# A hybrid SSD and attention layer on one core: w_down's operands prepared after the products with w_up in the first half, and that half's second norm as two fused VectorE passes

## The chip, the cores and the metric

The kernel runs on one core of a Trainium2 chip. The metric is the device time of one execution in microseconds (us). The comparison is with the median of three runs of the kernel before.

## The reference

One step of a one-layer encoder is computed for a prompt of 2048 frames and a sample of 64 frames, each frame a row of 1024 numbers, all in float32:

```
mix = token_mixers(x)                      # SSD heads and windowed attention, projections w_in and w_out
h = LN1(alpha * x + mix)
y = LN2(alpha * h + (silu(h @ w_gate) * (h @ w_up)) @ w_down)
LN(r) = (r - mean) * rsqrt(var + eps) * g + b
```

w_gate and w_up are 1024 x 2816, w_down is 2816 x 1024. Besides y, the states of both mixers are returned. The change concerns the second half of the layer alone: the preparation of w_down, and LN2 on the first 1024 frames of the prompt.

## The kernel before

Every float32 operand of a large product is split into two float16 parts, a high and a low one, and a product is three TensorE matmuls (`mm3`, lines 127 to 129: high by high, high by low, low by high) into one PSUM bank. Before the split an operand is scaled by a power of two taken from its largest absolute value.

The feed-forward part runs in two halves of the prompt, `h` = 0 (blocks 0 to 3, 256 frames each, two row tiles of 128 frames per block) and `h` = 1 (blocks 4 to 7, with the sample). In each half a loop goes over `p` = 0 to 10, the pairs of 128 columns of w_gate and w_up, which are also pairs of 128 rows of w_down. One pass of the loop (lines 1362 to 1370) has these steps:

- `gate(p)`: seven products of 4 x 3 matmuls with w_gate's operands (a scheme of the Strassen-Winograd kind), then SiLU on ScalarE (ACT).
- `flush(pend)`: the products with w_down for the pass before, `down_rows`. Each of eight rows of 128 frames and each half of the columns has 6 matmuls into a bank `pds`, and VectorE (DVE) adds the bank to the accumulator `acc` in SBUF (line 1198).
- `get_w(h, p + 1, 0)`: in the first half `prep_w` loads the next pair of w_gate columns (1 MB, line 943) into a tile `raw`, takes its bound, and splits it into eight operands (ACT line 954, DVE line 955) that are also stored to HBM (line 956). The second half loads these again (`load_ws`).
- `get_w(h, p, 2)`: `prep_d` loads w_down's rows of this pass (1 MB, line 990), takes the bound, and splits them into the operands `wd`: four in the first half, eight in the second.
- `up(h, p, groups)`: the seven products with w_up, their product with the gate, its bound, and the split into the operands `act` (lines 1143 and 1144).
- `get_w(h, p + 1, 1)`: the next pair of w_up columns.

A bound is taken thus: ACT sums absolute values into a column (line 935), DVE takes the larger of two columns (`am`, line 936) and casts it (line 80), TensorE spreads it over the partitions with a small matmul into the bank `pmx` (line 81, called the max product below), and DVE reduces the bank (line 82) and makes the scale from it (lines 92 to 95).

The raw tiles of w_gate, w_up and w_down share two buffers (`tag="raw", bufs=2`), so that a load waits until the split of the raw tile two loads earlier is done.

When the last pass of the first half has been multiplied with w_down, `last(rows, False)` (line 1281) normalizes the rows of blocks 0 to 3. DVE takes the mean and variance (lines 1296 and 1297) and the reciprocal root (`rsqrt1`, lines 113 to 123), and forms `nb` = -mean * root (line 1301). Then ACT applies scale and bias to the 128 x 1024 row tile (line 1311), DVE multiplies by g (line 1312), and GpSimd (POOL) adds b (line 1313). SyncE (SP) writes the tile out (line 1315) and the same buffer is loaded again for the second half (line 1190). At the end of the second half the rows go through two fused DVE passes instead (lines 1306 and 1308).

The order of the instructions on each engine is made by a scheduler when the program is built, from the order in which the program issues them, a simulated timeline and `tc.high_priority`. On the chip each engine runs its own list strictly in order.

Of the kernel before, what the change touches and what calls it, by code (L numbers as in the profile page):

```python
# [13 lines left out]
F32 = mybir.dt.float32  # L14
U32 = mybir.dt.uint32
I32 = mybir.dt.int32
AF = mybir.ActivationFunctionType
ALU = mybir.AluOpType
# [4 lines left out]
P = 128  # L23
# [26 lines left out]
def layer_kernel(ctx: ExitStack, tc: tile.TileContext, I, O, consts):  # L50
    nc = tc.nc
    V, S, G, T, Q = nc.vector, nc.scalar, nc.gpsimd, nc.tensor, nc.sync

    cp = ctx.enter_context(tc.tile_pool(name="cp", bufs=1))
    small = ctx.enter_context(tc.tile_pool(name="small", bufs=4))
# [29 lines left out]
    def max3():  # L85
        return psx[0].tile([P, P], F32, tag="max", name="pmx")
# [10 lines left out]
    def absmax(out, in_):  # L97
        ax = {2: AX.X, 3: AX.XY, 4: AX.XYZ}[len(in_.shape)]
        V.tensor_reduce(out=out, in_=in_, op=ALU.max, axis=ax, apply_absolute_value=True)
# [809 lines left out]
    def b_tiles(pool_, h, order):  # L909
        return {i: pool_.tile([P, 4, 2, 4, P], F16, tag="B", bufs=len(order), name=f"B{h}_{i}") for i in order}  # L910
# [107 lines left out]
    def scheme(h, p):  # L1018

        return h == 1 and p < NP_ - 2  # L1020

    def load_ws(p, m, order):
        wts[p, m] = w_tiles(p, m, order)
        for i in order:
            Q.dma_start(out=wts[p, m][i], in_=wsd[p][m][i])

    def get_w(h, p, m):
        if p >= NP_:
            h, p = h + 1, 0
        if h == 2:  # L1030
            return
        if m == 2:
            prep_d(h, p)
        elif h == 0:
            prep_w(p, m)
        else:
            load_ws(p, m, ORD + (0,))
# [3 lines left out]
    gb = {}  # L1041
# [15 lines left out]
    def products_sample(w):  # L1057

        ps = psp.tile([P, 2, DSEQ], F32, tag="p", name="pss")
        for f in range(2):  # L1060
            for kk in range(2):
                a = w[((1, 2), (0, 4))[f][kk]]
                for k in range(4):
                    mm3(ps[:, f], a[:, 0, k], a[:, 1, k], sB[:, kk, 0, k], sB[:, kk, 1, k],
                        start=(kk + k == 0), stop=(kk == 1 and k == 3))
        return ps
# [51 lines left out]
    def up(h, p, groups):  # L1118
        iu = invs[:, p, 1:2]
        for g in groups:  # L1120
            am = small.tile([P, 4], F32, tag="ama", name="ama")
            if g.sub:
                o = g.sg
                V.scalar_tensor_tensor(out=o, in0=products_sample(wts[p, 1]), scalar=iu, in1=o,
                                       op0=ALU.mult, op1=ALU.mult)
                absmax(am[:, 0:1], o)
            else:
                s = products(wts[p, 1], g)
                for j, c in enumerate(CS):
                    o = s["5"] if c == "11" else s[c]  # L1130
                    V.scalar_tensor_tensor(out=o, in0=s[c], scalar=iu, in1=g.sg[c], op0=ALU.mult, op1=ALU.mult)
                    absmax(am[:, j:j + 1], o)
                    s[c] = o
                absmax(am[:, 0:1], am)
            asc = small.tile([P, 1], F32, tag="asc", name="asc")
            ai = small.tile([P, 1], F32, tag="ai", bufs=8, name="ai")
            scale_from(am[:, 0:1], ai, asc, 2.0 ** 11 if scheme(h, p) and not g.sub else 2.0 ** 13,
                       ps=max3())
            act = {}
            g.acts[p] = act, ai  # L1140

            def split(at, x):
                S.activation(at[:, 0], x, AF.Identity, scale=asc)  # L1143
                V.scalar_tensor_tensor(out=at[:, 1], in0=x, scalar=asc, in1=at[:, 0], op0=ALU.mult, op1=ALU.subtract)  # L1144

            def put(i, x):
                if g.nq == 4:
                    act[i] = p3r.tile([P, 2, 4, P], F16, tag="act", bufs=7, name="act")
                else:
                    if i % 2:  # L1150
                        two[0] = p3r.tile([P, 2, 2, 2, P], F16, tag="act", bufs=7, name="act2")
                    act[i] = two[0][:, (i - 1) % 2]
                split(act[i], x)

            two = [None]

            if g.sub:
                at = p3r.tile([P, 2, 2, DSEQ], F16, tag="acts", bufs=2, name="acts")
                split(at, o)
                for f in range(2):  # L1160
                    act[f] = at[:, :, f]
                continue

            a11, a12, a21, a22 = s["11"], s["21"], s["12"], s["22"]
            put(1, a11)
            if not scheme(h, p):
                put(2, a12)
                put(3, a21)
                put(4, a22)
                continue  # L1170
            put(4, a22)
            G.tensor_tensor(out=a22, in0=a21, in1=a22, op=ALU.add)
            G.tensor_tensor(out=a21, in0=a11, in1=a21, op=ALU.subtract)
            G.tensor_tensor(out=a11, in0=a22, in1=a11, op=ALU.subtract)
            put(6, a11)
            put(2, a12)
            put(7, a21)
            put(5, a22)
            G.tensor_tensor(out=a12, in0=a12, in1=a11, op=ALU.subtract)
            put(3, a12)  # L1180
# [100 lines left out]
    def last(rows, end):  # L1281

        b, n = rows[0][0], len(rows)
        L = P if b < NB else DSEQ
        mv = small.tile([P, 2, 2], F32, tag="mv", bufs=6, name="mv")[:L]
        rs = small.tile([P, 2], F32, tag="rs2", bufs=6, name="rs2")[:L, :n]
        nb = small.tile([P, 2], F32, tag="nb", name="nb")[:L, :n]
        with tc.high_priority(offset=PRI):
            for j, row in enumerate(rows):
                r = accs[row][:L]  # L1290
                if end and (b == 6 or j == 0 and b != 7):
                    row_stats(r, L, mv[:, j, 0:1], mv[:, j, 1:2])
                else:
                    bs = small.tile([P, 2, 6], F32, tag="bs", name="bs")
                    for c in range(2):
                        V.bn_stats(out=bs[:L, c], in_=r[:, c * 512:c * 512 + 512])
                    V.bn_aggr(out=mv[:, j], in_=bs[:L])
            for j in range(n):
                rsqrt1(mv[:, j, 1:2], LN_EPS / ALPHA ** 2, rs[:, j:j + 1], L)
                if not end:  # L1300
                    V.scalar_tensor_tensor(out=nb[:, j:j + 1], in0=mv[:, j, 0:1], scalar=-1.0, in1=rs[:, j:j + 1],
                                           op0=ALU.mult, op1=ALU.mult)
        for j, row in enumerate(rows):
            r = accs[row][:L]
            if end:
                V.scalar_tensor_tensor(out=r, in0=r, scalar=mv[:, j, 0:1], in1=gb[2][:L, 0],
                                       op0=ALU.subtract, op1=ALU.mult)
                V.scalar_tensor_tensor(out=r, in0=r, scalar=rs[:, j:j + 1], in1=gb[2][:L, 1],
                                       op0=ALU.mult, op1=ALU.add)
            else:  # L1310
                S.activation(r, r, AF.Identity, scale=rs[:, j:j + 1], bias=nb[:, j:j + 1])
                V.tensor_tensor(out=r, in0=r, in1=gb[2][:L, 0], op=ALU.mult)
                G.tensor_tensor(out=r, in0=r, in1=gb[2][:L, 1], op=ALU.add)
            c0 = b * BLK + j * P
            Q.dma_start(out=(O["y_p"].rearrange("b l d -> (b l) d")[c0:c0 + P] if b < NB else
                             O["y_s"].rearrange("b l d -> (b l) d")), in_=r)
# [36 lines left out]
    for h in range(2):  # L1353
        Bt = {**(b_tiles(p3, h, ORD[:5]) if h else B0), **b_tiles(p3r, h, ORD[5:])}
        for i in ORD:
            for q in range(4):
                if h or (q, i) not in direct:
                    Q.dma_start(out=Bt[i][:, q], in_=hd[4 * h + q][i])
        groups = [Group(Bt, blocks(4 * h, 4 * h + 4))]
        if h == 1:  # L1360
            groups.append(Group(sB, [[(NB, 0)]]))
        for p in range(NP_ - 2 if h else NP_):
            gate(p, groups)
            flush(pend)
            get_w(h, p + 1, 0)
            if p or h:
                get_w(h, p, 2)
            up(h, p, groups)
            get_w(h, p + 1, 1)
            pend = (p, groups)  # L1370


    p, p1 = NP_ - 2, NP_ - 1
# [21 lines left out]
    for g in (gs, ga):  # L1395
        for rows in g.rows:
            last(rows, True)
# [53 lines left out]
```

## Time and profile before

| | |
|---|---|
| median of three runs | 2293.24 us (2290.3 to 2294.82) |
| the profiled execution's own time | 2292.77 us |
| span from its first to its last instruction | 2291.0 us |
| TensorE busy | 2166.3 us, 95% |
| VectorE busy | 1778.9 us, 78% |
| ScalarE busy | 1031.2 us, 45% |
| GpSimd busy | 439.6 us, 19% |
| granted clock of TensorE, mean | 0.983 |

The span is 1.77 us shorter than the time of the execution. PE is TensorE, PEld its weight loads. In the trace a line such as L1198 is a line of the kernel before. After "<-" in brackets stands what ended an idle time.

### The profile page before, as it was taken

The page shows a single profiled execution, that of the slowest core. Times are in us where ns is not written, and L with a number is a line of the kernel's source. Part 1 is how long each engine was busy: PE and PEld are TensorE (multiplying, and loading weights), DVE is VectorE, ACT ScalarE, POOL GpSimd, SP SyncE. Part 2 cuts the span into 40 slices and gives each one's busy share as a digit, 9 for nine tenths or more (in the row PEclk, how much of TensorE's full clock was granted, in tenths as well). Part 3 has the DMA queues.
Part 4 walks back from the last instruction along what each step waited for, and adds up shares of the span by engine and source line. Part 5 has one row for each costly group of instructions (what it writes and reads, how often), then busy time and mean ns, then how long its engine had stood idle before and what let it go on. Part 6 is the DMA issues. An engine that isn't in the chain of part 4 may idle for free.

```text
span 2291.0 us, 38739 instructions
## 1 busy us (share of the span) xinstructions
PE 2166.3 (95%) x14805; PEld 1295.6 (57%) x14805; DVE 1778.9 (78%) x4389; ACT 1031.2 (45%) x2040; POOL 439.6 (19%) x388
## 2 busy tenths in 40 slices
PE   5898999999999999989999999999889999999996
PEld 5787778777875555434444444444344444444674
DVE  7786887797778768477777877776987877777978
ACT  5444544554474657644444444432233333333331
POOL 2111211111112002022222222211322222222400
PEclk9899999999999999999999999999999999999998
DMA  7001000100032557643333333345442222222431
GB/s 225 15 26 32 26 19 34 33 24 25 35 98 96 190 170 275 230 146 131 114 126 124 136 132 129 129 163 209 166 144 91 91 87 81 93 81 84 144 109 74
DMA packets 139774, 248.33 MB, mean 108 GB/s; under 512 B 21184, under 2 KB 54212, under 8 KB 139588
## 3 DMA queue, kind: packets, MB, share of 16 engines
q1 hardware_dynamic: 139588, 245.86, 31.9%
q8 instruction: 116, 1.90, 0.3%
q14 instruction: 70, 0.57, 0.1%
HBM read 161.90 MB, written 83.91 MB: 107 GB/s over the span
## 4 chain that ended last, share of the span: by engine, by line
PE 58%; DVE 21%; issue 8%; DMA 6%; ACT 5%; POOL 2%; SPq 0%; DVEq 0%; ACTq 0%; POOLq 0%
PE ps L129 7%; PE ps L127 7%; PE ps L128 7%; PE mm L127 4%; PE mm L129 4%; PE mm L128 3%; DVE w L955 3%; DMA raw<-in_w_up 2%; PE pd L127 2%; PE pd L129 2%; PE pd L128 2%; PE pso L127 2%; PE pso L128 2%; PE pso L129 2%; DVE cc L449 2%
## 5 line engine op out<-in xcount | busy, mean ns | idle before, releaser
L127 PE MATMUL ps<-B,w 128*128 128x512 f16 (+1 forms) x1344 | 486.0, 363 | 14.4 <-ACT a L1086 8.7
L128 PE MATMUL ps<-B,w 128*128 128x512 f16 (+1 forms) x1344 | 487.7, 363 | 0.0
L129 PE MATMUL ps<-B,w 128*128 128x512 f16 (+1 forms) x1344 | 485.0, 363 | 0.0
L128 PEld LDWEIGHTS <-w 128*128 128x128 f16 x2920 | 284.3, 99 | 170.2 <-issue 27.7
L129 PEld LDWEIGHTS <-w 128*128 128x128 f16 x2920 | 284.9, 99 | 157.3 <-issue 8.3
L127 PEld LDWEIGHTS <-w 128*128 128x128 f16 x2920 | 284.5, 99 | 157.7 <-issue 8.9
L127 PE MATMUL mm<-x,w 128*128 128x256 f16 (+1 forms) x1224 | 315.1, 268 | 6.5 <-ACT w L254 2.2
L129 PE MATMUL mm<-x,w 128*128 128x256 f16 (+1 forms) x1224 | 314.8, 268 | 1.3 <-DVE w L257 1.3
L128 PE MATMUL mm<-x,w 128*128 128x256 f16 (+1 forms) x1224 | 315.3, 268 | 0.0
L1198 DVE SCALAR_TENSOR_TENSOR acc<-pds,ai,acc 128x512 f32<-128x512 f32 x208 | 152.8, 742 | 33.9 <-PE pds L129 33.7
L1198 DVE SCALAR_TENSOR_TENSOR acc<-pd,ai,acc 128x512 f32<-128x512 f32 x216 | 151.0, 739 | 26.9 <-PE pd L129 26.0
L955 DVE SCALAR_TENSOR_TENSOR w<-raw,fsc,w 128x512 f16<-128x512 f32 x176 | 150.6, 895 | 20.9 <-ACT w L954 20.9
L127 PE MATMUL pds<-wd,act 128*128 128x512 f16 x416 | 158.1, 380 | 7.4 <-DVE acc L1198 6.5
L128 PE MATMUL pds<-wd,act 128*128 128x512 f16 x416 | 158.1, 380 | 0.0
L129 PE MATMUL pds<-wd,act 128*128 128x512 f16 x416 | 157.4, 380 | 0.0
L1090 POOL TENSOR_TENSOR a<-a 128x512 f32<-128x512 f32 (+1 forms) x48 | 59.6, 1241 | 460.9 <-ACT a L1089 408.7
L1001 ACT ACTIVATE wd<-rawd,fsc 128x512 f16<-128x512 f32 x124 | 83.5, 715 | 138.0 <-PE pd L129 70.6
L954 ACT ACTIVATE w<-raw,fsc 128x512 f16<-128x512 f32 x176 | 114.1, 710 | 66.4 <-POOL raw L963 30.3
L1143 ACT ACTIVATE act<-a,asc 128x512 f16<-128x512 f32 (+1 forms) x123 | 76.4, 683 | 117.1 <-DVE asc L94 111.5
L128 PEld LDWEIGHTS <-act 128*128 128x128 f16 x668 | 65.5, 98 | 87.2 <-issue 14.9
L127 PEld LDWEIGHTS <-act 128*128 128x128 f16 x668 | 65.5, 98 | 81.6 <-ACT act L1143 5.3
L129 PEld LDWEIGHTS <-act 128*128 128x128 f16 x668 | 65.3, 98 | 80.5 <-DVE act L1144 1.8
(378 smaller groups left out, 4331.0 us busy)
## 6 DMA issues: line engine op xcount, KB each, us to landing
w<-ws SPq DMA_DIRECT2D x204, 256.0 KB, 3.0
ws<-w SPq DMA_DIRECT2D x176, 256.0 KB, 2.1
rawd<-in_w_down SPq DMA_DIRECT2D x22, 1024.0 KB, 5.0
x<-in_x_prompt SPq DMA_DIRECT2D x32, 512.0 KB, 4.2
raw<-in_w_gate SPq DMA_DIRECT2D x11, 1024.0 KB, 5.3
raw<-in_w_up SPq DMA_DIRECT2D x11, 1024.0 KB, 5.5
hd<-ht SPq DMA_DIRECT2D x41, 256.0 KB, 2.1
B<-hd SPq DMA_DIRECT2D x41, 256.0 KB, 5.4
```

The costliest lines, as they stand in the source:

```text
L127: T.matmul(out, lh, rh, start=start, stop=False, **kw)
L128: T.matmul(out, lh, rl, start=False, stop=False, **kw)
L129: T.matmul(out, ll, rh, start=False, stop=stop, **kw)
L449: V.scalar_tensor_tensor(out=cc[:, c], in0=cin[:, c, k:k + n], scalar=CW(k, ch + c), in1=cc[:, c], op0=ALU.mult, op1=ALU.add)
L954: S.activation(w[i][:, 0], x, AF.Identity, scale=sc)
L955: V.scalar_tensor_tensor(out=w[i][:, 1], in0=x, scalar=sc, in1=w[i][:, 0], op0=ALU.mult, op1=ALU.subtract)
L1001: S.activation(w[i][:, 0], x, AF.Identity, scale=sc)
L1090: G.tensor_tensor(out=s["7"], in0=s["7"], in1=s["5"], op=ALU.add)
L1143: S.activation(at[:, 0], x, AF.Identity, scale=asc)
L1198: V.scalar_tensor_tensor(out=acc[:, cs], in0=ps, scalar=ai, in1=acc[:, cs], op0=ALU.mult, op1=ALU.add)
```

## The change

Two edits. In the first half, `get_w(h, p, 2)` is issued after `up` and no longer ahead of it (passes 1 to 10; pass 0 has its w_down from ahead of the loop). And `last` always takes the two fused DVE passes, so that `nb`, the ACT pass and the POOL pass go.

```diff
@@ def last(rows, end):
-        nb = small.tile([P, 2], F32, tag="nb", name="nb")[:L, :n]
...
-                if not end:
-                    V.scalar_tensor_tensor(out=nb[:, j:j + 1], in0=mv[:, j, 0:1], scalar=-1.0, in1=rs[:, j:j + 1],
-                                           op0=ALU.mult, op1=ALU.mult)
         for j, row in enumerate(rows):
             r = accs[row][:L]
-            if end:
-                V.scalar_tensor_tensor(out=r, in0=r, scalar=mv[:, j, 0:1], in1=gb[2][:L, 0],
-                                       op0=ALU.subtract, op1=ALU.mult)
-                V.scalar_tensor_tensor(out=r, in0=r, scalar=rs[:, j:j + 1], in1=gb[2][:L, 1],
-                                       op0=ALU.mult, op1=ALU.add)
-            else:
-                S.activation(r, r, AF.Identity, scale=rs[:, j:j + 1], bias=nb[:, j:j + 1])
-                V.tensor_tensor(out=r, in0=r, in1=gb[2][:L, 0], op=ALU.mult)
-                G.tensor_tensor(out=r, in0=r, in1=gb[2][:L, 1], op=ALU.add)
+            V.scalar_tensor_tensor(out=r, in0=r, scalar=mv[:, j, 0:1], in1=gb[2][:L, 0],
+                                   op0=ALU.subtract, op1=ALU.mult)
+            V.scalar_tensor_tensor(out=r, in0=r, scalar=rs[:, j:j + 1], in1=gb[2][:L, 1],
+                                   op0=ALU.mult, op1=ALU.add)
@@ the loop over p
             get_w(h, p + 1, 0)
-            if p or h:
+            if h:
                 get_w(h, p, 2)
             up(h, p, groups)
+            if p and not h:
+                get_w(h, p, 2)
             get_w(h, p + 1, 1)
```

What the scheduler makes of it is seen in the order of the instructions. The first place is DVE in pass 2 of the first half, where w_down's bound is taken and its operands are split; `am_13766` and `a_13773` are the maxima of w_down of that pass. Before:

```order
L1083 TENSOR_TENSOR a<-ps,a 128x512
L955 SCALAR_TENSOR_TENSOR w_3_3_13715<-raw_3_13706,fsc,w_3_3_13715 128x512
L1198 SCALAR_TENSOR_TENSOR acc_1_13093<-pds,ai,acc_1_13093 128x512 x2
L936 TENSOR_TENSOR am_13766<-am_13766 128x1
L80 CAST a_13773<-am_13766 128x1
L1198 SCALAR_TENSOR_TENSOR acc_0_13127<-pds,ai,acc_0_13127 128x512 x2
L82 TENSOR_REDUCE pm<-pmx 128x1
L92 TENSOR_SCALAR pb<-pm 128x1
L94 TENSOR_SCALAR fsc<-pb 128x1
L95 RECIPROCAL invs<-fsc 128x1
L997 TENSOR_SCALAR invs<-invs 128x1
L936 TENSOR_TENSOR am_13935<-am_13935 128x1
```

With the change (`a_13875` is the maximum of the pass's activations, `a_13908` that of w_down, `a_13942` that of the next w_up):

```order
L80 CAST a_13875<-ama 128x1
L80 CAST a_13908<-am_13901 128x1
L80 CAST a_13942<-am_13935 128x1
L1083 TENSOR_TENSOR a<-ps,a 128x512
L1198 SCALAR_TENSOR_TENSOR acc_1_13165<-pds,ai,acc_1_13165 128x512
L82 TENSOR_REDUCE pm<-pmx 128x1
L92 TENSOR_SCALAR pb<-pm 128x1
L94 TENSOR_SCALAR asc<-pb 128x1
L95 RECIPROCAL ai<-asc 128x1
L1144 SCALAR_TENSOR_TENSOR act<-a,asc,act 128x512 x4
L82 TENSOR_REDUCE pm<-pmx 128x1
L92 TENSOR_SCALAR pb<-pm 128x1
```

The cast of w_down's maximum and its max product stood alone in the middle of the products with w_up, close behind the load. They now stand behind the maximum of the activations, and the split of w_down follows the split of the activations. On TensorE the max product of w_down moves in each of the ten passes from 93 to 195 matmuls ahead of that of the activations to 20 to 29 behind it.

The second place is DVE in the norm of the first half, at the second row tile. Before (`nb` feeds ACT, `gb` holds g and b):

```order
L122 SCALAR_TENSOR_TENSOR rsw_18208<-rs_18187,mv 128x1
L1296 BN_STATS bs<-acc_0_13091 128x6
L123 SCALAR_TENSOR_TENSOR rs_18187<-rsw_18208,rs_18187 128x1
L1297 BN_AGGR mv<-bs 128x2
L1301 SCALAR_TENSOR_TENSOR nb<-mv,rs_18187 128x1
L116 TENSOR_SCALAR mv<-mv 128x1
L117 TENSOR_SCALAR rs_18260<-mv 128x1
L119 TENSOR_SCALAR rs_18260<-rs_18260 128x1
L122 SCALAR_TENSOR_TENSOR rsw_18270<-rs_18260,mv 128x1
L123 SCALAR_TENSOR_TENSOR rs_18260<-rsw_18270,rs_18260 128x1
L122 SCALAR_TENSOR_TENSOR rsw_18270<-rs_18260,mv 128x1
L123 SCALAR_TENSOR_TENSOR rs_18260<-rsw_18270,rs_18260 128x1
```

With the change (L1301 and L1303 are the two fused passes in the new file):

```order
L1198 SCALAR_TENSOR_TENSOR acc_0_13091<-pds,ai,acc_0_13091 128x512
L116 TENSOR_SCALAR mv<-mv 128x1
L1301 SCALAR_TENSOR_TENSOR acc_1_13057<-acc_1_13057,mv,gb 128x1024
L1295 BN_STATS bs<-acc_0_13091 128x6
L117 TENSOR_SCALAR rs_18187<-mv 128x1
L1198 SCALAR_TENSOR_TENSOR acc_0_13091<-pds,ai,acc_0_13091 128x512
L119 TENSOR_SCALAR rs_18187<-rs_18187 128x1
L1295 BN_STATS bs<-acc_0_13091 128x6
L122 SCALAR_TENSOR_TENSOR rsw_18206<-rs_18187,mv 128x1
L1296 BN_AGGR mv<-bs 128x2
L123 SCALAR_TENSOR_TENSOR rs_18187<-rsw_18206,rs_18187 128x1
```

The first fused pass needs the mean alone and runs ahead of the root; the second follows when the root is there. Nothing of this norm stands on ACT's and POOL's lists any more.

## Rows read from the trace of the kernel before

**Rows 1.** The page's part 1: busy time, share and instructions of each engine.

```profile
PE 2166.3 (95%) x14805; PEld 1295.6 (57%) x14805; DVE 1778.9 (78%) x4389; ACT 1031.2 (45%) x2040; POOL 439.6 (19%) x388
```

**Rows 2.** Windows by stage: length, busy PE, PEld, DVE, ACT, POOL, clock, DMA.

```profile
1100.00:1589.00 489.00, 485.25 (x2305) 220.50 (x2304) 366.17 (x687) 221.07 (x368) 109.00 (x77) 1.00 0.41 145
1589.00:1690.00 101.00, 84.79 (x484) 38.95 (x483) 99.31 (x209) 31.78 (x45) 37.70 (x20) 0.93 0.45 154
1690.00:2190.00 500.00, 496.53 (x3608) 262.50 (x3607) 394.72 (x732) 165.71 (x277) 119.94 (x93) 1.00 0.31 98
```

**Rows 3.** Waits of PE, 1000 to 1100 us: us in total, times, longest.

```profile
PE pmx L81 <- DVE a L80: 5.1, 2, 3.4
```

**Rows 4.** Timeline around 1088 us, by engine: start, duration, instruction, idle before it.

```profile
1077.11 0.39 SPq L990 DMA_DIRECT2D rawd<-in_w_down  x1
...
1085.85 1.06 ACT L935 ACTIVATE wd<-rawd 128x1024 f16<-128x1024 f32 x1 [5.28 <-DMA rawd<-in_w_down]
...
1088.21 0.16 DVE L936 TENSOR_TENSOR am<-am 128x1 f32<-128x1 f32 x1 [5.27 <-ACT wd L935]
...
1088.62 0.29 PE L81 MATMUL pmx<-ident,a 128*128 128x128 bf16 x1 [3.39 <-DVE a L80]
```

**Rows 5.** Window 1080 to 1100 us, columns as in rows 2.

```profile
1080.00:1100.00 20.00, 16.61 (x72) 7.08 (x70) 10.37 (x23) 8.47 (x15) 1.51 (x1) 0.91 0.49 164
```

**Rows 6.** Waits of PE, 1100 to 1589 us, all of them.

```profile
PE ps L127 <- ACT a L1089: 1.3, 3, 0.5
PE pds L127 <- DVE acc L1198: 1.2, 4, 0.4
PE ps L127 <- ACT a L1086: 1.0, 1, 1.0
```

**Rows 7.** Timeline of PE, two matmuls of 128x512 that follow each other.

```profile
1590.59 0.38 PE L127 MATMUL ps<-B,w 128*128 128x512 f16 x1
1590.81 0.38 PE L128 MATMUL ps<-B,w 128*128 128x512 f16 x1
```

**Rows 8.** Lines 943 and 990, loads of w_gate and w_up, then w_down.

```profile
DMA to landing us min/median/max: 5.1/5.5/8.3
...
DMA to landing us min/median/max: 4.7/5.0/5.8
```

**Rows 9.** Timeline of DVE, the split of w_down in one pass.

```profile
1095.18 2.74 DVE L1002 SCALAR_TENSOR_TENSOR wd<-rawd,fsc,wd 128x512 f16<-128x512 f32 x4 [0.45 <-ACT wd L1001]
```

**Rows 10.** Lines of DVE, 1589 to 1690 us: count, busy us, mean ns, idle before.

```profile
L1312 DVE TENSOR_TENSOR acc<-acc,gb 128x1024 f32<-128x1024 f32 x8 | 9.7, 1217 | 0.1
...
L1301 DVE SCALAR_TENSOR_TENSOR nb<-mv,rs 128x1 f32<-128x1 f32 x8 | 3.2, 404 | 0.0
```

**Rows 11.** Lines of POOL, 1589 to 1690 us, the addition of b.

```profile
L1313 POOL TENSOR_TENSOR acc<-acc,gb 128x1024 f32<-128x1024 f32 x8 | 19.7, 2468 | 41.1 <-DVE nb L1301 22.1 <-DVE acc L1312 12.0 <-issue 4.1
```

**Rows 12.** Timelines of POOL and DVE beside its passes: second; first, second, eighth.

```profile
1613.12 2.34 POOL L1313 TENSOR_TENSOR acc<-acc,gb 128x1024 f32<-128x1024 f32 x1 [4.92 <-DVE acc L1312]
...
1606.42 1.80 DVE L123 SCALAR_TENSOR_TENSOR rs<-rsw,rs 128x1 f32<-128x1 f32 x1
1613.21 2.27 DVE L123 SCALAR_TENSOR_TENSOR rs<-rsw,rs 128x1 f32<-128x1 f32 x1
1670.26 3.49 DVE L1144 SCALAR_TENSOR_TENSOR act<-a,asc,act 128x512 f16<-128x512 f32 x2
```

**Rows 13.** Lines 123 and 1144 over the whole span: ns min/median/max.

```profile
L123 DVE SCALAR_TENSOR_TENSOR rs<-rsw,rs x51: 99/145/2270, 1594.1 to 2283.5; 128x1 f32<-128x1 f32 x48, 64x1 f32<-64x1 f32 x3
...
L1144 DVE SCALAR_TENSOR_TENSOR act<-a,asc,act x123: 464/746/2845, 994.9 to 2263.1; 128x512 f16<-128x512 f32 x107, 128x256 f16<-128x256 f32 x16
```

**Rows 14.** Line 1306, the fused pass at the end of the second half.

```profile
L1306 DVE SCALAR_TENSOR_TENSOR acc<-acc,mv,gb x8: 1264/1270/1272, 2216.8 to 2278.9; 128x1024 f32<-128x1024 f32 x8
```

**Rows 15.** Waits, 1550 to 1720 us and (PE) 1589 to 1690 us.

```profile
ACT acc L1311 <- DVE nb L1301: 27.4, 7, 6.4
...
PE ps L127 <- ACT a L1086: 3.8, 1, 3.8
```

## The prediction

> **What bounds the kernel now.** The page comes first: TensorE is busy 95% of the span, VectorE 78% [rows 1]. These are averages, so the stages that the change touches are read one by one, with the windows. From 1100 to 1589 us, most of the first half's loop, PE is busy 485.25 of 489 us at full clock: TensorE bounds it, and at most 3.75 us are to be had there [rows 2]. From 1589 to 1690 us, where the first half is normalized and the second begins, it is the other way round: PE is busy 84.79 of 101 us at a mean clock of 0.93, and DVE 99.31 of 101 us. DVE bounds this stretch, and PE waits 16.2 us in it. From 1690 us on PE is full again (496.53 of 500), so that whatever is won or lost earlier is carried to the end undiminished.
>
> Next, the waits of PE, stage by stage. From 1000 to 1100 us there are two that matter, 5.1 us together, of the small matmul that spreads a maximum [rows 3]. The timeline of the longer one shows its cause from the first to the last step: SP issues the load of w_down at 1077.11, ACT has waited 5.28 us when it lands at 1085.85, DVE has waited 5.27 us when it takes the maximum, and PE stands 3.39 us at the max product [rows 4]. PE's list is strictly ordered, so a max product that comes early stops everything behind it. The same 20 us have a mean clock of 0.91 where full is 1.00 (the two levels are 2.4 and 1.2 GHz) [rows 5]. From 1100 to 1589 us PE waits only 3.5 us in all, and for no max product [rows 6].
>
> **Part A: w_down behind the products with w_up.** Each of the ten moved steps issues one load on SP, the bound on ACT and DVE, one max product on PE, four splits on ACT and four on DVE; nothing on POOL in this half. No instruction is added. What changes is the places in the lists.
>
> What goes: both waits of rows 3 belong to w_down's max product, which now stands 20 to 29 matmuls behind that of the activations. The load is long done there. Gain 5.1 us. With the wait goes the fall of the clock behind it: 0.09 of 20 us below full means 3.6 us at half rate, by the two levels, and so 1.8 us of lost work if PE had been at it all the time; part of these 3.6 us it only waited, so I take half, 0.9 us. Together **-6.0 us**.
>
> What is late next: first, the split itself. By the order, w_down's first product follows its max product after 20 to 27 matmuls. Two matmuls stand 0.22 us apart [rows 7], so that is 4.3 to 5.8 us. In that time DVE makes the scale (about 1 us), finishes up to four splits of the activations, and makes the first split of w_down; four splits take 2.74 us and start 0.45 us behind ACT [rows 9]. That is 1 + 2.7 + 1.2 = 4.9 us at the worst: short by 0.6 us or with 0.9 us to spare. Second, the two raw buffers: the next w_gate load now waits for this split. From w_down's max product to w_gate's there are 72 to 77 matmuls, 15.5 to 16.6 us. The chain is the scale 1 us, the splits 3.2 us, the issue 0.4 us, the load, two sums on ACT of some 1.1 us each, and maximum and cast 0.4 us; with the load at its median of 5.5 us [rows 8] that is 12.7 us, and up to a microsecond more if DVE is still at the activations. With the slowest load, 8.3 us, it is 15.5 to 16.5 us and PE would begin to wait. Behind a waiting max product on PE stands all work; behind a late bound on DVE stand the additions that free PSUM banks for PE.
>
> So the new waits are bounded by nothing and by about 1.5 us in each of ten passes, 15 us. The nearest row is the loop as it stands, where loads of the same size run through a chain of the same kind and no max product waits [rows 6]. I stay near the low end, **+2.0 us**.
>
> **Part B: two fused passes.** Eight row tiles. DVE loses eight multiplications, 9.7 us, and eight `nb` of about 0.14 us where nothing is in their way, 1.1 us [rows 10]. It gets sixteen fused passes of 1.27 us, priced by the same pass at the end of the second half [rows 14]: 20.3 us. On paper that is +9.5 us on the engine that bounds.
>
> The trace has another cost of the old way. While POOL adds b, 2.34 us from 1613.12, an operation of DVE on one number per partition takes 2.27 us [rows 12], where the median of its kind is 0.145 us [rows 13]. It begins with POOL's pass and ends with it. Beside each of POOL's eight passes one or more DVE operations are stretched so, of kinds that otherwise take 0.15 to 0.7 us; the first is stretched to 1.80 us, and the last pair, two splits, to 3.49 us where two take some 1.4 [rows 12, 13]. Over what their kinds take elsewhere the eight are 1.6 to 2.2 us too long, 15.5 us in all. POOL's passes are 19.7 us [rows 11], which is the most that they can have cost; below, I allow 0.7 us each, a third of what is seen, if the delay would otherwise come from something else.
>
> The Trainium skill (SBUF — State Buffer, section Who interferes with whom) says that GpSimd shares one pair of SBUF ports with VectorE, held as an exclusive lock, and that a VectorE instruction with two SBUF inputs waits for a GpSimd instruction that reads SBUF. The rows agree, down to the one-column operations. By that rule the whole of POOL's passes would come back to DVE, and the sum would be 4 us better.
>
> Sum of part B on DVE: +20.3 - 9.7 - 1.1 - 15.5 = **-6.0 us**, between -10.2 (with 19.7) and +3.9 (with 5.6). Since DVE is busy 98% of the stretch, I take it whole. The eight ACT passes cost nothing by themselves, but ACT waits 27.4 us for `nb` with its list behind it, and PE once 3.8 us for an ACT copy [rows 15]; this goes with them, inside the same DVE-bound time, so I add nothing. In the second pair of buffers, the load of w_down for the second half now waits for the split of pass 10, as above: 79 matmuls, 17 us, against some 13; no cost. The rows are written out earlier or at the same place of the list; the reload of the accumulators follows that.
>
> **Sum.** -6.0 + 2.0 - 6.0 = -10.0 us. The profiled execution took 2292.77 us, 0.5 us less than the median of the runs, so I forecast **2283 us**.
>
> **The rivals.** *The waits only move.* Part A's 5.1 us come back as waits of the split or of the w_gate load: 0.8 us in each of ten passes, 8 us instead of 2, and part B yields half, -3. Then -6 + 8 - 3 = -1, 2292 us. For it: loads took up to 8.3 us [rows 8], and the spare time is 1 to 3 us. Against it: TensorE's list was laid out anew with the later places, and the loop has held such a layout with 3.5 us lost in 489.
>
> *DVE becomes the longer bound.* The stretched operations would have met other work of POOL anyway (it is busy 37.7 us there, 19.7 of them for b [rows 2, 11]), so that nothing of the 15.5 us returns. Then the stretch grows by 20.3 - 9.7 - 1.1 = 9.5 us, and with part A the time is 2292.8 - 4.0 + 9.5 = 2298 us. It decides against the change as soon as less than 5.5 us return, 0.7 us per pass. For it: DVE is the fullest engine there, and two lighter ones are relieved in its place. Against it: in the rows the stretched operation begins and ends with the addition of b. The Trainium skill (Perfetto Trace Analysis, section Optimizing Scalar/DVE Operations) speaks for this rival: where VectorE is saturated, offloading work to ScalarE or even GpSimd may make sense, and the change does the reverse. The same section adds that between VectorE and GpSimd it might not help, and rows 12 stand on that side.
>
> **How the numbers follow.** I give the forecast 0.66, the waits that only move 0.2, the longer bound 0.12, and 0.02 to anything else. About 0.2%, 4.6 us, is what a measurement of this kernel can tell from no change; faster then means under 2288.7 us, slower over 2297.8. The forecast's own range, with part B from -10.2 to -3 and new waits from 0 to 5 us, is 2276.6 to 2288.8. The whole range goes up to the case of moved waits, 2276 to 2294, and leaves out the slower rival and the ends. Faster 0.65, same 0.23, slower 0.12.
>
> **What would show it.** In the new profile no max product should wait from 1000 to 1100 us, and the clock there should stay at 1.00. In the loop PE should lose no more than some 6 us in ten passes; waits on a max product or on ScalarE's splits of w_down there would be the first rival. In the stretch after the loop POOL's passes of 128x1024 are gone, no one-column operation of DVE takes over 1.5 us except beside POOL's remaining work, and from the last gate of the first block of rows to full PE the stretch is some 95 us where it was 101. If DVE is full there for 105 us or more, part B is wrong; if the fused passes take much more than 1.27 us, its price is.

## The result and the profile after

The changed kernel takes **2268.27 us** (median of four runs, 2267.45 to 2269.7), the kernel before beside it 2292.55 us: ratio **0.989**, 95% interval 0.9876 to 0.9904, 22 to 28 us faster. The forecast was 2283 us, 10 us faster; the result lies 8 us below the lower end of the range. The profiled execution took 2269.7 us, its span is 2267.9.

The page's part 1 of the changed kernel answers to [rows 1]:

```profile
PE 2160.3 (95%) x14805; PEld 1295.3 (57%) x14805; DVE 1764.3 (78%) x4389; ACT 1024.0 (45%) x2032; POOL 421.9 (19%) x380
```

The shares have not moved, so the stages have to be compared. Fixed times don't serve for that once one kernel runs ahead of the other. Both traces hold 14805 matmuls in nearly the same order, so I cut both at the same matmuls, counted from the start: number 7358 (in the first half's loop, while the lists are still the same), 10093 (where the norm begins) and 11334 (in the second half, where the distance of the two kernels stands still). These are the windows of the kernel before, between those cuts; the columns are those of rows 2:

```profile
1000.10:1590.10 590.00, 580.31 (x2736) 262.38 (x2735) 444.21 (x823) 268.07 (x446) 137.91 (x96) 1.00 0.41 144
1590.10:1800.10 210.00, 193.79 (x1243) 93.10 (x1242) 180.43 (x357) 68.22 (x105) 61.41 (x38) 0.97 0.36 123
```

The same work in the changed kernel:

```profile
1003.10:1583.60 580.50, 576.87 (x2737) 262.47 (x2736) 437.90 (x823) 270.21 (x446) 138.02 (x96) 1.00 0.43 146
1583.60:1777.90 194.30, 188.10 (x1243) 91.65 (x1242) 173.30 (x360) 60.01 (x98) 42.84 (x30) 0.98 0.38 133
```

The 23.1 us between the two spans are: +3.0 before the first cut, where the two programs are the same (a chance difference, see the last section), **-9.5 in the loop**, **-15.7 in the norm** and what follows it, -0.9 behind. The forecast was -4.0 for the first and -6.0 for the second.

*The loop.* The waits of PE in the changed kernel, 1003 to 1584 us, all of them, answer to [rows 3, 6]:

```profile
PE pds L127 <- DVE acc L1198: 2.1, 5, 0.6
PE ps L127 <- ACT a L1086: 1.1, 1, 1.1
PE ps L127 <- ACT w L954: 0.2, 1, 0.2
```

No max product waits any more, and no wait for w_down's splits has come in. How far one execution can be trusted here is known: eleven kernels of this document, all that have part A in all ten passes of the first half, have the same lists in the loop, and their executions took 579 to 585 us for it, with PE idle for 2.3 to 5.8 us. The window of [rows 5] now reads full clock and a full PE, though DVE is at work for 13.76 of the 20 us:

```profile
1080.00:1100.00 20.00, 20.00 (x95) 9.06 (x93) 13.76 (x21) 8.49 (x14) 7.57 (x5) 1.00 0.66 222
```

*The norm.* DVE's lines between the second and the third cut, first before, then changed, both with the same number of splits and root steps (columns as in rows 10):

```profile
L1144 DVE SCALAR_TENSOR_TENSOR act<-a,asc,act 128x512 f16<-128x512 f32 x21 | 22.8, 1115 | 2.2 <-ACT act L1143 2.2
...
L122 DVE SCALAR_TENSOR_TENSOR rsw<-rs,mv 128x1 f32<-128x1 f32 x24 | 10.2, 430 | 0.1
L1312 DVE TENSOR_TENSOR acc<-acc,gb 128x1024 f32<-128x1024 f32 x8 | 9.7, 1217 | 0.1
L123 DVE SCALAR_TENSOR_TENSOR rs<-rsw,rs 128x1 f32<-128x1 f32 x24 | 8.2, 350 | 0.2
```

```profile
L1144 DVE SCALAR_TENSOR_TENSOR act<-a,asc,act 128x512 f16<-128x512 f32 x21 | 16.4, 809 | 2.2 <-ACT act L1143 2.2
...
L1301 DVE SCALAR_TENSOR_TENSOR acc<-acc,mv,gb 128x1024 f32<-128x1024 f32 x8 | 10.9, 1363 | 0.0
L1303 DVE SCALAR_TENSOR_TENSOR acc<-acc,rs,gb 128x1024 f32<-128x1024 f32 x8 | 10.6, 1331 | 0.0
L122 DVE SCALAR_TENSOR_TENSOR rsw<-rs,mv 128x1 f32<-128x1 f32 x24 | 4.8, 207 | 0.0
L123 DVE SCALAR_TENSOR_TENSOR rs<-rsw,rs 128x1 f32<-128x1 f32 x24 | 4.3, 187 | 0.0
```

The root's one-column steps and the splits of the activations are 15.7 us shorter without having changed (5.4 + 3.9 + 6.4): most of what POOL's passes had cost stood there. Smaller lines go both ways: `nb`, now gone, had taken 2.1 us more than its price, lines 936 and 1097 took 2.9 us less together, and w_down's splits (L1002) took 2.9 us more. The two fused passes take 21.5 us, a little above their price of [rows 14].

And yet DVE's busy time in the window fell by 7.1 us only (180.43 to 173.30), while the window shrank by 15.7. So the other 8.6 us are *idle* time of DVE: 29.6 us before, 21.0 now. That is the part the forecast did not have. The windows can be split where DVE stops being full, first before, then changed:

```profile
1590.10:1690.00 99.90, 83.69 (x479) 38.47 (x478) 98.66 (x209) 31.78 (x45) 37.70 (x20) 0.93 0.44 153
1690.00:1800.10 110.10, 110.10 (x766) 54.63 (x765) 81.77 (x149) 36.44 (x60) 23.71 (x18) 1.00 0.30 96
```

```profile
1583.60:1673.00 89.40, 83.27 (x504) 39.43 (x503) 89.20 (x208) 23.14 (x38) 19.61 (x12) 0.96 0.43 150
1673.00:1777.90 104.90, 104.83 (x740) 52.22 (x739) 84.10 (x153) 36.87 (x60) 23.23 (x18) 1.00 0.34 119
```

DVE's idle time lies in the second rows, where PE is full: 28.3 us before, 20.8 changed. In the first rows, with DVE full, the changed kernel gets 504 of PE's matmuls done in 89.4 us, the kernel before 479 in 99.9; what is left over there PE has to do afterwards, while DVE idles. PE's waits show what held it up. From 1575 to 1720 us the changed kernel has a single one, where [rows 15] and its timeline before had waits up to 1682 us:

```profile
PE pd L127 <- ACT act L1143: 6.1, 1, 6.1
```

The timeline, PE at the end of this wait and DVE around and behind it:

```profile
1647.66 0.61 PE L127 MATMUL pd<-wd,act 128*128 128x512 f16 x1 [6.13 <-ACT act L1143]
...
1649.16 1.27 DVE L1301 SCALAR_TENSOR_TENSOR acc<-acc,mv,gb 128x1024 f32<-128x1024 f32 x1
...
1664.93 1.27 DVE L1303 SCALAR_TENSOR_TENSOR acc<-acc,rs,gb 128x1024 f32<-128x1024 f32 x1
...
1667.47 1.28 DVE L1303 SCALAR_TENSOR_TENSOR acc<-acc,rs,gb 128x1024 f32<-128x1024 f32 x1
```

Three of the sixteen passes come after PE has started again, and DVE stays full until 1673 us without holding PE up. In the kernel before, the last L1312 stand at 1663.78 and 1669.07 us, *ahead* of the splits and additions that PE needs, and POOL's last pass stretches those splits to 3.49 us [rows 12]:

```profile
1663.78 1.22 DVE L1312 TENSOR_TENSOR acc<-acc,gb 128x1024 f32<-128x1024 f32 x1
...
1669.07 1.21 DVE L1312 TENSOR_TENSOR acc<-acc,gb 128x1024 f32<-128x1024 f32 x1
...
1670.26 3.49 DVE L1144 SCALAR_TENSOR_TENSOR act<-a,asc,act 128x512 f16<-128x512 f32 x2
...
1676.87 0.73 DVE L1198 SCALAR_TENSOR_TENSOR acc<-pd,ai,acc 128x512 f32<-128x512 f32 x1
```

```profile
1682.12 0.38 PE L127 MATMUL pd<-wd,act 128*128 128x512 f16 x1 [0.51 <-DVE acc L1198]
```

PE's clock goes along. In windows of 20 us it was short of full by 0.06, 0.02, 0.17 and 0.09 from 1600 to 1680 us before, 6.8 us in all, and by 0.17 in one window after, 3.4 us. Each of these falls stands within a wait of PE or close behind one. It is the same time seen from PE's side, and isn't added to the above.

### The profile page after: what moved, and what is told of

Its sections match the earlier page's. It is cut to its first block, busy times and chain, and to the rows that moved or that the text cites. A ratio compares the mean times of both kernels' runs of the same rounds, so it can differ in the third digit from the quotient of the medians.

```text
span 2267.9 us, 38738 instructions
## 1 busy us (share of the span) xinstructions
PE 2160.3 (95%) x14805; PEld 1295.3 (57%) x14805; DVE 1764.3 (78%) x4389; ACT 1024.0 (45%) x2032; POOL 421.9 (19%) x380
## 4 chain that ended last, share of the span: by engine, by line
PE 70%; DVE 18%; issue 4%; ACT 4%; DMA 3%; POOL 1%; SPq 0%; DVEq 0%; ACTq 0%; POOLq 0%
PE ps L129 9%; PE ps L127 9%; PE ps L128 9%; PE mm L127 4%; PE mm L129 4%; PE mm L128 4%; PE pds L127 3%; PE pds L128 3%; PE pds L129 3%; PE pso L127 2%; PE pso L128 2%; PE pso L129 2%; PE pd L127 2%; PE pd L128 2%; PE pd L129 2%
```

## The experiments

All twelve, in the order in which they say something. The ratio is to the kernel before on the same chip; the changed kernel's is 0.989. "Window" is the one between the second and the third cut; since the profiled executions scatter ahead of the first cut, stages are read from there and verdicts from the ratio.

**Do the parts add up?** Part A alone (the loop's edit, old `last`):

```diff
-            if p or h:
+            if h:
                 get_w(h, p, 2)
             up(h, p, groups)
+            if p and not h:
+                get_w(h, p, 2)
```

> Part A alone; the norm of the first half is the old one. The landmarks of the changed profile stand 6.8 us earlier at the end of the first half's loop, so if the parts add up this takes 2285.7 us (2292.5 - 6.8), within 2 us, and TensorE's waits in the stretch of the norm stay near 16 us. If the two parts help each other in that stretch (w_down of pass 10 is now split there), it is off this by more than 4 us in either direction.

Measured: 2282.75 us, ratio 0.9947 (0.9935 to 0.9959), 12 us. And part B alone (new `last`, the loop as before):

> Part B alone. If the parts add up: 2292.5 - 16 to -17 = 2276 us, within 2 us, with the two waits of max products from 1000 to 1100 us still there. If the gain in the norm needs part A: 2280 us or more.

Measured: 2279.46 us, ratio 0.9939 (0.9926 to 0.9953), 14 us. 12 and 14 make 26 where both together make 25: the parts add up. A alone missed its own forecast, though, 12 us for 6.8: that was read from the landmarks of the two profiles, which hold the 3.0 us by which the changed kernel's execution came later to the first cut. B's 2279.46 us lies between its two outcomes; its interval, 11 to 17 us, does not rule out the 16 to 17 that were expected. Loop and window of part A alone, then of part B alone:

```profile
1000.20:1579.30 579.10, 576.64 (x2736) 262.43 (x2735) 435.96 (x823) 269.68 (x446) 138.13 (x96) 1.00 0.43 147
1579.30:1788.40 209.10, 194.86 (x1243) 94.07 (x1241) 178.57 (x357) 68.23 (x106) 61.60 (x38) 0.95 0.38 124
```

```profile
998.60:1589.90 591.30, 581.15 (x2737) 263.07 (x2736) 444.67 (x823) 268.39 (x446) 137.85 (x96) 0.99 0.42 144
1589.90:1787.40 197.50, 189.41 (x1242) 92.45 (x1241) 175.93 (x360) 59.62 (x98) 40.93 (x30) 0.98 0.40 131
```

Part A gives 10.9 us in the loop and 0.9 in the norm, part B nothing in the loop and 12.5 us in the norm. In the norm that makes 13.4 of the 15.7 us; whether the parts help each other by the rest, or it is chance between single executions, no run decides. DVE's busy time in the window falls by 1.8 us with part A alone (180.43 to 178.57) and by 4.5 with part B alone.

**What did POOL's passes cost?** Part A and the old norm with POOL's addition on DVE:

```diff
-                G.tensor_tensor(out=r, in0=r, in1=gb[2][:L, 1], op=ALU.add)
+                V.tensor_tensor(out=r, in0=r, in1=gb[2][:L, 1], op=ALU.add)
```

> Part A and the old norm, with the addition of b moved from POOL to VectorE; the pass on ScalarE stays. Against part A alone, VectorE gets 8 additions of 1.22 us (+9.7) and loses what POOL's passes held it up by. Theory 1 (POOL's passes hold VectorE for their length, and that is most of part B's gain): 6 to 10 us faster than part A alone, some 2276 to 2280 us, although work is added to the bound engine. Theory 2 (what counts is that the trip over ScalarE and its waits are gone, or TensorE's order): not faster than part A alone, up to 10 us slower, 2286 to 2296 us.

Measured: 2274.3 us, ratio 0.9922 (0.9906 to 0.9938), 8.5 us under part A alone by the medians: theory 1. The window:

```profile
1589.60:1791.70 202.10, 188.89 (x1242) 92.60 (x1241) 172.22 (x365) 68.01 (x105) 43.24 (x30) 0.97 0.38 128
```

DVE got 9.9 us of additions and was busy 6.4 us *less* than in part A alone (178.57 to 172.22). POOL's eight passes had cost it 16.3 us; the forecast had 15.5. The other way round, the changed kernel with a POOL pass put back:

```diff
             V.scalar_tensor_tensor(out=r, in0=r, scalar=rs[:, j:j + 1], in1=gb[2][:L, 1],
                                    op0=ALU.mult, op1=ALU.add)
+            if not end:
+                G.tensor_tensor(out=r, in0=r, in1=gb[2][:L, 1], op=ALU.add)
```

> The changed kernel with one more pass on POOL per row tile of the first half, behind the second fused pass (it adds b a second time, so the first half's y_p is not the reference's). VectorE's list gets nothing, and only the write-out waits for the pass. Theory 1: operations of VectorE beside the eight passes are stretched again, +15 us or more, 2283 us. Theory 2: nearly free, 2268 to 2271 us.

Measured: 2281.12 us, ratio 0.9941 (0.9929 to 0.9953), 12 us slower than the changed kernel. Theory 2 falls, but the price is below what theory 1 had: DVE is busy 9.1 us more, not 15.

```profile
1585.20:1789.30 204.10, 190.45 (x1243) 91.91 (x1242) 182.40 (x360) 60.31 (x98) 64.23 (x38) 0.97 0.39 127
```

The timelines say why the same passes cost less here. First two of the eight on POOL, then what DVE does beside them:

```profile
1608.43 2.35 POOL L1306 TENSOR_TENSOR acc<-acc,gb 128x1024 f32<-128x1024 f32 x1 [1.16 <-DVE acc L1303]
1621.06 2.35 POOL L1306 TENSOR_TENSOR acc<-acc,gb 128x1024 f32<-128x1024 f32 x1 [10.28 <-DVE rs L117]
```

```profile
1608.41 0.74 DVE L1198 SCALAR_TENSOR_TENSOR acc<-pds,ai,acc 128x512 f32<-128x512 f32 x1
1609.07 2.27 DVE L1097 TENSOR_TENSOR a<-a 128x512 f32<-128x512 f32 x1
...
1620.97 0.67 DVE L1096 TENSOR_TENSOR a<-ps,a 128x512 f32<-128x512 f32 x1
1621.57 0.73 DVE L1198 SCALAR_TENSOR_TENSOR acc<-pds,ai,acc 128x512 f32<-128x512 f32 x1
1622.23 0.68 DVE L1295 BATCH_NORM_STATS2 bs<-acc 128x6 f32<-128x512 f32 x1
...
1623.14 0.82 DVE L1131 SCALAR_TENSOR_TENSOR a<-a,invs 128x512 f32<-128x512 f32 x1
```

Beside the second pass DVE goes on at its usual pace: two operations with one operand in PSUM, and one with a single operand. Beside the first, `a<-a`, with two operands in SBUF, takes 2.27 us instead of 0.68: it stands until the pass is over and ends 0.6 us behind it. So a pass costs what is left of it when DVE comes to an operation with two operands in SBUF. In the old norm such an operation came at once beside each of the eight passes, a step of the root beside three of them, and each was 1.6 to 2.1 us too long; here the eight passes cost from nothing to 2.2 us each.

**Is a microsecond of DVE a microsecond of the kernel here?** The changed kernel with one more DVE pass per row tile (`V.tensor_tensor(out=r, in0=r, in1=gb[2][:L, 1], op=ALU.add)` in the place of the POOL pass above):

> The changed kernel with one more pass of VectorE per row tile of the first half, behind the second fused pass (it adds b a second time, so the first half's y_p is not the reference's): 8 passes of 1.22 us, 9.7 us of VectorE's time, and neither ScalarE nor POOL gets anything. It measures what a microsecond of VectorE is worth in this stretch. If one for one, as the prediction had it: 2278 us. If each microsecond costs more, through waits that set TensorE's clock back: 2282 us or more. If passes that fall behind TensorE's last wait are free: 2271 to 2275 us.

Measured: 2276.87 us, ratio 0.9929 (0.9915 to 0.9943), 9 us over the changed kernel. The window grows by 10.1 us, DVE's busy time by 10.8: one for one, as the forecast took it.

```profile
1586.70:1791.10 204.40, 189.15 (x1242) 92.82 (x1241) 184.09 (x367) 60.21 (x98) 43.11 (x30) 0.97 0.38 127
```

**Where do the other 8.6 us come from?** Between the run with the addition on DVE and the changed kernel DVE's busy time is the same to 1.1 us, but the windows differ by 7.8 (202.10 and 194.30). What differs is the trip over ACT, with the eight `nb` that feed it. Two runs split it. First an ACT pass that nothing on DVE waits for, behind the second fused pass:

```diff
+            if not end:
+                S.activation(r, r, AF.Identity)
```

> The changed kernel with a pass of ScalarE per row tile of the first half behind the second fused pass; it copies the tile onto itself. VectorE's list gets nothing and waits for nothing new; ScalarE's list gets eight passes of 1.24 us that wait for VectorE with ScalarE's other work behind them. Theory 3 (the part of B's gain that POOL's passes don't explain, some 8 us between the run with the addition on VectorE and the changed kernel, was ScalarE's list standing behind the norm): 5 to 8 us slower than the changed kernel, 2274 to 2277 us. Theory 4 (it was VectorE, whose second pass stood behind the trip over ScalarE): within 2 us of the changed kernel, 2267 to 2271 us.

Measured: 2268.43 us, ratio 0.9883 (0.9867 to 0.99): no difference. ACT's list standing behind the norm costs nothing; theory 3 falls. Then the trip in the middle:

```diff
-            V.scalar_tensor_tensor(out=r, in0=r, scalar=rs[:, j:j + 1], in1=gb[2][:L, 1],
-                                   op0=ALU.mult, op1=ALU.add)
+                S.activation(r, r, AF.Identity, scale=rs[:, j:j + 1])
+                V.tensor_tensor(out=r, in0=r, in1=gb[2][:L, 1], op=ALU.add)
```

> The changed kernel with the trip over ScalarE put back between two passes of VectorE: VectorE makes (x - mean) * g, ScalarE multiplies by the root, VectorE adds b. VectorE's work is the same to 0.5 us, POOL has none of it. Theories 3 and 4 both expect the 8 us back, 2275 to 2279 us; if it comes to 2270 us or less, the trip costs nothing, and the 8 us were the eight small operations for the bias of ScalarE's pass or the order of the list.

Measured: 2274.1 us, ratio 0.9903 (0.9886 to 0.9919), about 3 us over the changed kernel, less than expected; the intervals overlap, so I lean on the window. It is 4.7 us longer although DVE is busy 2.1 us *less*:

```profile
1585.50:1784.50 199.00, 188.71 (x1242) 92.40 (x1241) 171.19 (x357) 68.14 (x105) 42.54 (x30) 0.98 0.40 130
```

PE waits 10.3 us there, where the changed kernel has its single wait of 6.1. The long wait, for the splits of the activations, is there in both; the small ones behind it are those that the changed kernel is rid of. The longest:

```profile
PE pdt L127 <- ACT acts L1143: 7.0, 1, 7.0
PE pd L127 <- DVE acc L1198: 2.3, 4, 0.9
```

Now nine kernels can be put side by side: length of the window, DVE busy in it, and the rest.

| kernel | window | DVE busy | DVE idle |
|---|---|---|---|
| before: trip over ACT | 210.0 | 180.4 | 29.6 |
| part A alone: trip | 209.1 | 178.6 | 30.5 |
| addition on DVE: trip | 202.1 | 172.2 | 29.9 |
| ACT in the middle: trip | 199.0 | 171.2 | 27.8 |
| part B alone: no trip | 197.5 | 175.9 | 21.6 |
| POOL pass back: no trip | 204.1 | 182.4 | 21.7 |
| one more DVE pass: no trip | 204.4 | 184.1 | 20.3 |
| changed: no trip | 194.3 | 173.3 | 21.0 |
| ACT pass behind: no trip | 193.6 | 172.9 | 20.7 |

Whatever DVE's work is, from 171 to 184 us, the idle time is 20 to 22 us without the trip and 28 to 31 with it. Of the five kernels below, all without the trip, four have 21 to 22.7 us; the fifth, with part A in the second half too, has 37, from waits of its own. DVE's work counts one for one, and the trip costs 6 to 10 us beside it. These are single executions, but the medians agree: the ratio's difference to the changed kernel less that of DVE's busy time leaves 8 us for the addition on DVE and 5 for ACT in the middle. PE's clock does not separate the two groups: it is 0.98 both in the run with ACT in the middle and in the changed kernel, and 0.97 in the one with one more DVE pass. That the cause is the place which the late passes then take in DVE's list, ahead of the splits and additions for the second half, is read from the timelines; the scheduler lays out all lists anew with every edit, so no run isolates the place alone. Two tried to. The norm written out behind the products with w_up:

> The changed kernel with the norm of the first half written behind the products with w_up of the second half's first pass, so that the scale and the split of its activations, for which TensorE stood 6.13 us in the changed kernel, need not share VectorE with the fused passes. If VectorE's order, not its amount of work, sets that wait: 4 to 8 us faster than the changed kernel, 2260 to 2264 us. If the amount of work does, or the reload of the accumulators now comes late and takes the place of that wait: no faster than 2266 us.

Measured: 2269.82 us, ratio 0.9884 (0.9867 to 0.9901), no difference. It tells little about the place: the scheduler gave PE the same list and DVE nearly the same. It does say how well a window repeats: 193.7 us here, 194.3 in the changed kernel. And the scale of the next activations with precedence:

> The changed kernel with the scale of the activations of the second half's first pass (the maximum, two bit operations, the reciprocal) given precedence in the order. In the changed kernel its three small operations on VectorE stood 5 and 2 us apart behind work of the norm, and TensorE waited 6.13 us for the split behind them. If the place in VectorE's list sets that wait: 3 to 6 us faster than the changed kernel, 2262 to 2266 us. If the adds and splits that are now later cost TensorE the same: within 2 us of it.

Measured: 2268.74 us, ratio 0.9889 (0.9874 to 0.9903), no difference: PE's wait is 5.5 us instead of 6.1, and no other is listed in the window, as in the changed kernel. The time is that of the second outcome, but its reason is not seen: the place of these small operations hardly moves the wait. What does stays open.

**Was part A two waits, or a better layout of all passes?** Part B whole, part A in passes 1 and 2 alone:

```diff
-            if h:
+            if h or p > 2:
                 get_w(h, p, 2)
             up(h, p, groups)
-            if p and not h:
+            if p in (1, 2) and not h:
                 get_w(h, p, 2)
```

> Part B whole, part A in passes 1 and 2 alone, those with the two waits for a max product. If part A's gain is those waits and the clock behind them, it keeps all but 1 us of it: 2267 to 2270 us. If, as the landmarks say, some 4 us of it come in small pieces from the passes behind 1100 us: 2271 to 2275 us.

Measured: 2282.07 us, ratio 0.9939 (0.9927 to 0.9952): nothing is left of part A's gain, which neither outcome had foreseen. The long waits for a max product are gone, but the loop takes 592.7 us (590.0 before), since PE now waits elsewhere, with eight passes at the old place and the loop's lists laid out anew:

```profile
PE ps L127 <- ACT a L1086: 6.7, 6, 2.0
PE pds L127 <- DVE acc L1198: 4.5, 9, 0.7
```

ACT's timeline ahead of one of them (PE waits 1.55 us there) shows the same mechanism one load further: ACT stands at the bound of the next w_up until its load lands, and the copy that frees PE's bank stands behind it.

```profile
1318.23 1.06 ACT L935 ACTIVATE w<-raw 128x1024 f16<-128x1024 f32 x1 [6.97 <-DMA raw<-in_w_up]
...
1320.47 0.58 ACT L1086 ACTIVATE a<-ps 128x512 f32<-128x512 f32 x1
```

**Two tries for a better version.** Part A in the second half too (`if p or h: get_w(h, p, 2)` behind `up`):

> The changed kernel with part A in the second half too. TensorE is busy 497.7 of 500 us there, so at most some 3 us are to be had; 2265 to 2269 us if the later place is harmless there as well, 2275 us or more if the eight operands of w_down there (four of them through POOL) come too late for the products.

Measured: 2337.32 us, ratio 1.019 (1.0177 to 1.0203), far slower. Waits of PE from 1720 to 2240 us:

```profile
PE pdt L129 <- DVE wd L1002: 28.5, 23, 2.1
PE pd L128 <- DVE wd L1002: 5.7, 8, 1.7
PE pdt L127 <- ACT wd L1001: 3.0, 1, 3.0
```

There w_down has eight operands to be split (in nine of the eleven passes), four of them by way of POOL, and the first products wait for them in eight passes, one after another. Whether the number of operands or the way over POOL is to blame, this run does not separate. Then the eight POOL operations of 128x512 that fall into the norm on DVE (`V` for `G` where `p == 0`, in the sums of w_down's and of the activations' quarters):

> The changed kernel with the eight POOL operations of the second half's first pass that fall into the norm (the sums of w_down's and of the activations' quarters, 128x512, 13.8 us of POOL in the changed kernel's trace) given to VectorE, 8 x 0.68 = 5.4 us of it. If POOL's operations there hold VectorE for most of their length, as its passes for b did, more comes back than is added: 0 to 6 us faster than the changed kernel, 2262 to 2268 us. If they mostly fall beside operations that aren't held: up to 5 us slower, 2268 to 2274 us.

Measured: 2275.42 us, ratio 0.9908 (0.989 to 0.9926), some 4 us slower, though the intervals touch: DVE got 5.4 us and is busy 2.2 us more in the window (175.53), so 3.2 us came back of POOL's 13.8. No run beats the changed kernel by more than the intervals.

## Why the prediction was wrong, step by step

- **Part A, what goes (-6.0):** right in kind. The waits for w_down's max product are gone and the clock stays full in [rows 5]. The clock's term was half of what it should be: the 3.6 us at half rate begin as the wait ends, and PE was at work nearly all through them, so they cost 1.8 us and not 0.9.
- **Part A, new waits (+2.0):** wrong, and the failing step of this part. The sum held w_down's chain against the time to its first use and left 0.6 us short. No such wait came, and the term measured nothing: PE's idle time in the loop apart from max products was 4.6 us before (9.7 less 5.1) and 3.6 with the change, and over the eleven kernels with the same lists it is 2.3 to 5.8 us, with 4.6 in the middle. Some 1.7 us more of PE's busy time went than the clock explains. An estimate accounts for half of it: within a stream a matmul takes up 0.22 us, ahead of a wait its full 0.38 [rows 7], and the waits listed in the loop fell from 12 to 7, which makes 0.8 us. The rest stays open.
- **Part B, DVE's sum (-6.0):** right in kind and near in size. DVE's busy time fell by 7.1 us; part B's own share of that is 4.5 (alone) to 5.3 (on top of part A). The fused passes took 1.2 us more than their price. The term for POOL's passes, 15.5 us, measured 15.7 by the lines and 16.3 by its own run; a microsecond of DVE is worth one here. From the rule of the Trainium skill (SBUF — State Buffer, section Who interferes with whom) the prediction read that POOL's whole passes would come back, 19.7 us; the runs show 16.3 in the old list and 9.1 in the new one. The rule tells which DVE operations wait; how long they do is set by when the next of them comes.
- **Part B, "so I add nothing" for ACT's trip:** the step that failed. [Rows 15] had ACT waiting 27.4 us for `nb`, and I asked only who waits behind ACT. The run with an ACT pass behind the norm shows that this indeed costs nothing. What costs is the way through ACT. By the timelines it makes DVE's own passes late, and they then stand ahead of the work that PE needs next; no run isolates that place. It is 8.6 us in the window, none of it in the sum or in the range. DVE was 98% busy in the stretch that I read, so an idle time of DVE had no place in the argument; it lies behind that stretch, where PE does what it was kept from by its waits up to 1682 us.
- **The rivals:** "The waits only move" came true for neither part, but for the loop with two passes moved it did. "DVE becomes the longer bound" fell: all of the 15.5 us returned. The Trainium skill (Perfetto Trace Analysis, section Optimizing Scalar/DVE Operations) stood behind that rival where it says that offloading work from a saturated VectorE may make sense. Here it did not, for either helper: POOL's passes stretched DVE, by 16.3 us (for GpSimd the same section has its doubts), and ACT's made DVE's own late, for 6 to 10 us.
- **The range:** it was made from the terms that I had and missed the one that I had put at nothing.

## What to carry to other kernels

Where an engine is full, price a step that leaves it and returns in two parts: the work it saves there, and the delay of what comes back, which then stands ahead of the next stage's work. Compare two kernels between the same matmuls, and split each stage into busy and idle time of the bounding engine: here the busy time followed the forecast and the idle time held what was missed. A step moved in some passes of a loop changes the lists of all: here moving it in two passes of ten lost the whole gain. And a place that serves one half can be ruinous where the step is twice as large.

## What the runs showed that was not expected

- POOL's pass over 128x1024 does not slow DVE as a whole. Operations with one operand, or with one of two in PSUM, run at their usual 0.67 to 0.74 us beside it; one with two operands in SBUF waits until it ends, even one of a single column (2.27 us for 0.145 [rows 12, 13]). The same eight passes cost DVE 16.3 us in one list and 9.1 in another.
- Executions of the same instructions scatter ahead of the change. All kernels here have the same lists up to the first cut, and reach it between 998.6 and 1006.3 us; the granted clock falls at different moments in them. The run with the addition on DVE is the extreme: its profiled execution took 2284.85 us where its median is 2274.3. Without the cuts, its trace would have spoken against the theory that its median supports.
